# Down projection in four groups of output tiles, one visit behind each pair of up tiles

## The chip, the cores and the metric

The kernel runs on one core of one Trainium2 chip. The metric is the device time of one execution in microseconds (us). TensorE multiplies matrices, VectorE and ScalarE do elementwise work, GpSimd and SyncE mostly issue transfers, and sixteen DMA engines move the data. In the profile these are PE (PEld is its weight load), DVE, ACT, POOL and SP.

## The reference

One layer of a decoder on 512 prompt tokens and 8 x 4 sample tokens, all in float32. The part that matters here is the second half of the layer.

```python
x = x + g1 * (jnp.concatenate([a_out, o], axis=-1) @ p['w_out'])
h2 = rms_norm(x, p['norm_ffn_g']) * (1 + sc2) + sh2
u, f_tail = causal_dwconv(f_prev, h2 @ p['w_up'], p['ffn_conv_w'], p['ffn_conv_b'])
gate, val = jnp.split(u, 2, axis=-1)
x = x + g2 * ((jax.nn.silu(gate) * val) @ p['w_down'])
```

D_MODEL is 2048 and D_FF is 5632. The six modulation vectors (`sh1` ... `g2`) are `silu(c) @ w_ada + b_ada`. The convolution has three taps along the tokens.

## The kernel before

Channels lie on the 128 partitions, tokens on the free axis: 544 columns as two halves of 272 (256 prompt tokens and 16 sample tokens each). Every float32 product is made of three float32r matmuls: weights and operands are split into a rounded part and a rest, `hi` by a ScalarE cast (L353) and `lo` by a VectorE subtraction (L354), and `hi*hi`, `hi*lo` and `lo*hi` are summed in PSUM. A weight unit of 512 KB (128 x 1024) is loaded by SyncE into a ring of five buffers (`raw_w` three, `raw_x` two), and `split_w` (L199) splits half of it at a time into a ring of three `whi` and three `wlo`.

Entry. While the output projection (`rest`, L832) runs, SyncE loads the weights of the last modulation stage, which holds the gate `g2`, into `raw_g`; the sixteen steps of the stage (`ada_stage`, L268) come after it, six ahead of the sum of squares and ten behind. `normalized` (L879) scales two channel tiles of x at a time, `blocks` (L894) splits them into the operands B1 and B2. The first two pairs of up tiles (a gate tile f and its value tile 44+f) are made by plain products (`direct`, L936), with 192 matmuls a pair. `combine` (L899) makes the operands T1, T2, T3 and T4.

Up. The other 42 pairs use seven products (`product`, L1025) in place of eight, 24 matmuls of 272 columns each. `up_mm` (L1035) loads four units, forms four weight combinations on VectorE (L1045 to L1047, L1055) and adds the products up from five PSUM banks (pool `psf`, four buffers, `bank`) into `usg` and `usv`. `gated_act` (L1083) then makes the convolution, silu, the product and the split of the result; five results are kept.

Down. `down(c)` (L1105) takes four K tiles (a chunk) and all sixteen output tiles m: 24 matmuls per m into one of two PSUM pairs (`main_ps`), an eviction that multiplies by the gate (ScalarE L1118, VectorE L1119) into a ring `ym` of three, and a GpSimd transfer that adds `ym` to `o_y[m]` in memory (L1120). The order of work is four pairs, with `down(c-1)` behind the first of them, eleven times:

```python
for j in range(2 if c == 0 else 0, CHUNK):
    up_pair(CHUNK * c + j, st_in, tails, j)
    ...
    if c and j == 0:
        down(c - 1)
```

Copies of the two window caches (128 of 1 MB, memory to memory, L924) are issued behind some of the weight loads (`shift_cache`). The program is written in this order, and a scheduler that estimates when each instruction becomes ready sets the final order on every engine's queue; engines take their queues strictly in that order. `tc.issue_after(ins)` fixes that an instruction comes behind `ins` on the engine of `ins`.

Of the kernel before, what the change touches and what calls it, by code (L numbers as in the profile page):

```python
# [60 lines left out]
YM = 3  # L61
# [3 lines left out]
              [(48 + k, 64 + k, 4) for k in (0, 4, 8, 12)] + [(80, 84, 4), (88, 92, 4)])  # L65
D2D = (PAST - DT) * DC // 8
# [53 lines left out]
def build(ctx, tc, A):  # L120
# [147 lines left out]
    def ada_stage(psp, tmp, s, loaded=None, banks=None):  # L268
# [3 lines left out]
        ps = banks[:, 0] if banks is not None else psp.tile([P, 512], F32, name="x", bufs=XB)  # L272
# [15 lines left out]
        pt = banks[:, 1] if banks is not None else psp.tile([P, 512], F32, name="m")  # L288
# [543 lines left out]
    def rest():  # L832
# [4 lines left out]
        for m in range(2, KT):  # L837
            ps = main_ps()
            for h in range(1 if m < 8 else 0, 2):
                mm_unit(ps, A["w_out"][m, h], mhi, mlo, 8 * h, h == 0 or m < 8, h == 1)  # L840
                yield
# [52 lines left out]
    def blocks(h, j, n):  # L894
        src = x2[h][:, j:j + n].rearrange("p k c n -> p c k n")
        hi, lo = (b[:, :, j:j + n] for b in (B1, B2)[h])
        split(hi, lo, src)
# [52 lines left out]
    for j in range(0, 4, 2):  # L950
        normalized(0, j, 2)
# [25 lines left out]
    def us_tile(st_in, slot):  # L977
        us = fe.tile([P, UW], F32, name="us", bufs=2)
        seg = us[:, USEG:].rearrange("p (b w) -> p b w", w=2 + DT)
        nc.gpsimd.memset(us[:, 0:2], 0.0)  # L980
        nc.gpsimd.tensor_copy(seg[:, :, 0:2], st_in[:, slot])
        return us
# [19 lines left out]
    def placed(outs, st_in, j):  # L1002
        uss = [us_tile(st_in, 2 * j + i) for i in range(2)]
        for us, out in zip(uss, outs):
            for c in range(2):
                place(us, c, copied, out[c])
        return uss

    st_in = state_tile(0)
    us0 = placed(first, st_in, 0)  # L1010
    second = [main_ps(), main_ps()]
# [6 lines left out]
    direct(1, [[t[:, c] for c in range(2)] for t in second], while_sums)  # L1018
# [16 lines left out]
    def up_mm(f, usg, usv):  # L1035
        a11, _ = load_u(A["w_up"][f, 0])
# [85 lines left out]
    for c in range(NCHUNK):  # L1122
        if c:
            st_in = state_tile(c)
# [134 lines left out]
```

## Time and profile before

| | us |
|---|---|
| Three runs: median (lowest to highest) | 2735.04 (2724.3 to 2739.17) |
| Profiled execution, own time | 2729.78 |
| Its span | 2728.0 |
| TensorE busy in the span | 2583.4 |
| VectorE busy | 1677.4 |
| ScalarE busy | 1258.3 |
| Mean granted TensorE clock, share of full | 0.982 |

The span runs from the first to the last instruction of the profiled execution. Busy time of TensorE has modelled ends, so it says how long matmuls were in flight and not how fast they went. "A <- B" in a row means that A stood idle until B was done.

### The profile page before, as it was taken

Reading aid. Unit: us, or ns where it says so; the run is one execution under the profiler, and the core shown is the slowest. Engines: PE = TensorE matmul, PEld = TensorE weight load, DVE = VectorE, ACT = ScalarE, POOL = GpSimd, SP = SyncE. Lnnn points to the kernel's source line nnn. Section 1 sums busy time; section 2 is a strip of 40 time slices with the busy share of each in tenths; the row PEclk is TensorE's granted clock in tenths of the full one; section 3 lists DMA queues with packets and bytes.
Section 4 is the critical chain, followed back from the end, with each engine's and each line's share of the span. In section 5 each row is a group of like instructions: output and inputs, shape, how many; then the busy total and the mean of one; then the engine's idle time right before and its main releaser. Section 6 shows DMA issues by size and latency. Waiting matters only on the chain.

```text
span 2728.0 us, 51730 instructions
## 1 busy us (share of the span) xinstructions
PE 2583.4 (95%) x20597; PEld 2342.4 (86%) x20597; DVE 1677.4 (61%) x3029; ACT 1258.3 (46%) x2371; POOL 332.4 (12%) x624
## 2 busy tenths in 40 slices
PE   6999999999999999799999999999999999999998
PEld 5878677768777789699999999999999999999998
DVE  4678654644665333785767667585748484848573
ACT  4355455444455322554444445454435454544443
POOL 0000000000000000012121211112121212121212
PEclk8999999999999999899999999999999999999999
DMA  9884557676756453448576776767585849585856
GB/s 347 273 274 156 194 196 259 221 258 230 245 190 216 150 203 131 156 163 224 184 225 183 228 202 212 202 205 205 211 202 199 215 180 246 188 238 176 244 169 107
DMA packets 144482, 566.53 MB, mean 208 GB/s; under 512 B 18544, under 2 KB 28400, under 8 KB 141424
## 3 DMA queue, kind: packets, MB, share of 16 engines
q1 hardware_dynamic: 103744, 494.98, 52.4%
q0 software_dynamic: 25344, 49.03, 11.8%
q10 hardware_dynamic: 15152, 19.22, 2.0%
q8 instruction: 161, 2.64, 0.4%
q14 instruction: 81, 0.66, 0.1%
HBM read 503.18 MB, written 193.94 MB: 256 GB/s over the span
## 4 chain that ended last, share of the span: by engine, by line
PE 67%; DVE 12%; DMA 10%; issue 6%; ACT 3%; POOL 1%; SPq 0%; DVEq 0%; ACTq 0%; POOLq 0%
PE acc L209 38%; PE b L933 18%; DVE wlo L354 4%; DMA raw_w<-w_up 4%; PE x L280 3%; DMA o_y<-ym 3%; DMA raw_x<-w_up 2%; ACT whi L353 2%; DVE ca L1078 2%; PE x L714 2%; PE x L665 2%; PE m L523 1%; DVE us L992 1%; ACT ca L1076 1%; DMA raw_g<-w_ada 1%
## 5 line engine op out<-in xcount | busy, mean ns | idle before, releaser
L353 ACT CAST whi<-raw_w 128x512 fp32r<-128x512 f32 x650 | 399.2, 619 | 694.4 <-PE acc L209 468.3
L354 DVE TENSOR_TENSOR wlo<-raw_w,whi 128x512 fp32r<-128x512 f32 x650 | 443.0, 689 | 414.4 <-ACT whi L353 404.3
L209 PE MATMUL acc<-hhi,whi 128*128 128x272 f32 x1792 | 394.9, 299 | 10.8 <-ACT whi L353 6.7
L209 PE MATMUL acc<-hhi,wlo 128*128 128x272 f32 x1792 | 383.3, 293 | 0.1
L209 PE MATMUL acc<-hlo,whi 128*128 128x272 f32 x1792 | 381.8, 293 | 0.0
L209 PEld LDWEIGHTS acc<-hhi,whi 128*128 128x128 f32 x1792 | 284.0, 190 | 61.2 <-issue 40.2
L209 PE MATMUL acc<-ahi,whi 128*128 128x272 f32 x1408 | 297.9, 294 | 29.0 <-DVE ym L1119 27.9
L209 PEld LDWEIGHTS acc<-hhi,wlo 128*128 128x128 f32 x1792 | 285.0, 190 | 22.7 <-issue 20.9
L209 PEld LDWEIGHTS acc<-hlo,whi 128*128 128x128 f32 x1792 | 284.4, 190 | 21.0 <-issue 18.5
L209 PE MATMUL acc<-alo,whi 128*128 128x272 f32 x1408 | 295.1, 291 | 0.0
L209 PE MATMUL acc<-ahi,wlo 128*128 128x272 f32 x1408 | 294.3, 291 | 0.0
L353 ACT CAST whi<-raw_x 128x512 fp32r<-128x512 f32 x270 | 165.7, 620 | 235.8 <-PE b L933 115.1
L354 DVE TENSOR_TENSOR wlo<-raw_x,whi 128x512 fp32r<-128x512 f32 x270 | 183.2, 687 | 121.9 <-ACT whi L353 119.6
L209 PEld LDWEIGHTS acc<-ahi,whi 128*128 128x128 f32 x1408 | 224.4, 192 | 33.7 <-DVE ym L1119 32.5
L209 PEld LDWEIGHTS acc<-alo,whi 128*128 128x128 f32 x1408 | 225.3, 192 | 0.2 <-DVE alo L354 0.2
L209 PEld LDWEIGHTS acc<-ahi,wlo 128*128 128x128 f32 x1408 | 224.8, 191 | 0.0
L933 PE MATMUL b<-b2hi,whi 128*128 128x272 f32 x704 | 205.8, 292 | 9.9 <-ACT whi L353 9.9
L933 PE MATMUL b<-b2hi,wlo 128*128 128x272 f32 x704 | 205.8, 293 | 8.7 <-DVE wlo L354 8.6
L933 PE MATMUL b<-b1hi,wlo 128*128 128x272 f32 x704 | 205.5, 295 | 2.2 <-DVE wlo L354 2.2
L933 PE MATMUL b<-b1hi,whi 128*128 128x272 f32 x704 | 204.0, 292 | 1.3 <-ACT whi L353 1.0
L933 PE MATMUL b<-b1lo,whi 128*128 128x272 f32 x704 | 204.6, 292 | 0.1
L933 PE MATMUL b<-b2lo,whi 128*128 128x272 f32 x704 | 203.3, 289 | 0.0
(253 smaller groups left out, 5175.1 us busy)
## 6 DMA issues: line engine op xcount, KB each, us to landing
raw_s<-w_ada SPq DMA_DIRECT2D x176, 512.0 KB, 4.8
o_k_s<-cache_k SPq DMA_DIRECT2D x64, 1022.0 KB, 7.1
o_v_s<-cache_v SPq DMA_DIRECT2D x64, 1022.0 KB, 6.9
raw_w<-w_up SPq DMA_DIRECT2D x109, 512.0 KB, 4.3
o_y<-ym POOLq DMA_DIRECT2D x176, 272.0 KB, 5.2
raw_w<-w_in SPq DMA_DIRECT2D x80, 512.0 KB, 4.5
raw_x<-w_up SPq DMA_DIRECT2D x67, 512.0 KB, 4.3
raw_s<-kT_c SPq DMA_DIRECT2D x64, 448.0 KB, 4.4
```

What stands on the lines that cost most here:

```text
L209: nc.tensor.matmul(out[:, c, 0:HALF], lhsT=w, rhs=x[:, c, :], start=start and i == 0, stop=stop and i == 2)
L280: nc.tensor.matmul(ps[32 * j:32 * j + 9, 0:w], lhsT=silc[:, kt, :], rhs=t[:, c:c + w], start=kt == 0, stop=kt == KT - 1)
L353: nc.scalar.copy(hi, src)
L354: return nc.vector.tensor_tensor(lo, src, hi.bitcast(F32), op=ALU.subtract).ins
L523: nc.tensor.matmul(o_ps[rows[par], 0:P], lhsT=vt[:, kj, rows[par]], rhs=pts[par][:, P * kj:P * kj + P], start=kj == 0, stop=kj == qi, skip ...
L665: nc.tensor.matmul(s_ps[32 * g:32 * g + 32, 0:hk], lhsT=qb[:, 2 * g + o, n, :], rhs=ks[g], start=o == 0 and n == 0, stop=o == 1 and n == 1 ...
L714: nc.tensor.matmul(o_ps[32 * g:32 * g + 32, :], lhsT=pT[0:w, c0:c0 + 32], rhs=rhs[g], start=kt == 0, stop=kt == 7)
L933: nc.tensor.matmul(out[:, 0:HALF], lhsT=w, rhs=x, start=start and i == 0, stop=stop and i == 2, skip_group_check=True)
L992: nc.vector.tensor_tensor(out, ps, t, op=ALU.add)
L1076: nc.scalar.activation(acc, us[:, 0:UN], AF.Identity, bias=fw[:, m, 3:4], scale=fw[:, m, 0:1])
L1078: nc.vector.scalar_tensor_tensor(acc, us[:, j:j + UN], fw[:, m, j:j + 1], acc, op0=ALU.mult, op1=ALU.add)
```

## The change

The down projection is cut into 47 visits of four output tiles. Visit v takes group v mod 4 (tiles 4g to 4g+3) and K tiles up to v, at most four; the first three and the last three visits have fewer. After pair f the program makes visit f-1, and between its two weight units it loads three units of pair f+1 and forms two of its weight combinations. After the last pair four visits are left. The units are padded with zeros to full size.

In `up_mm` the products run in another order (B11, B21, T2, T1, T3, B22, T4), three banks take all seven (b1 four times, b3 twice), and partial results go from PSUM to SBUF by ScalarE copies. `usg` and `usv` are two fixed tiles, their sample heads written by ScalarE. The ring `ym` shrinks from three to two.

At the entry, one load of the last modulation stage is issued behind each weight load of the output projection from the seventh on, six steps of the stage run inside the projection, and five ahead of the sum. Normalisations other than the first two are issued behind splits on VectorE. The first direct pair uses the PSUM pairs of `main_ps`, the second the banks, and pair 2 borrows the former.

```diff
-YM = 3
+YM = 2
...
+VISITS = ([(f % CHUNK, max(0, f + 1 - CHUNK), min(f + 1, CHUNK)) for f in range(FT)] +
+          [(g, FT - CHUNK + g + 1, CHUNK - 1 - g) for g in range(CHUNK - 1)])
...
-    raw_g = []
+    raw_g = deque()
     loads = ada_loads(last_ada, lambda: og.tile([P, 1024], F32, name="raw_g"))
-    for i, _ in enumerate(rest()):
-        if i >= 10 and len(raw_g) < RAW_G:
-            raw_g.append(next(loads))
-
-    ada = ada_stage(psf, op, last_ada, chain(raw_g, loads), main_ps())
-    for _ in range(6):
+
+    def loaded():
+        while True:
+            yield raw_g.popleft()
+
+    ada = ada_stage(psf, op, last_ada, loaded(), [psf.tile([P, 512], F32, name="b") for _ in range(2)])
+    for i, ins in enumerate(rest()):
+        if ins is not None and i >= 6:
+            if i >= 18:
+                next(ada)
+            with tc.issue_after(ins):
+                t = next(loads, None)
+            if t is not None:
+                raw_g.append(t)
+
+    for _ in range(5):
...
+    todo = deque((h, j) for h in range(2) for j in range(0, 8, 2))
+    for _ in range(2):
+        normalized(*todo.popleft(), 2)
 
     def plain(h, u):
-        for j in (0, 2):
-            blocks(h, 4 * u + j, 2)
-            if (h, u) != (1, 1):
-                normalized(h + u, 4 * (1 - u) + j, 2)
-
-    first = [[bank(), bank()] for _ in range(2)]
-    direct(0, first, plain)
+        for j in (4 * u, 4 * u + 2):
+            ins = blocks(h, j, 2)
+            if todo:
+                with tc.issue_after(ins):
+                    normalized(*todo.popleft(), 2)
+
+    first = [main_ps(), main_ps()]
+    direct(0, [[t[:, c] for c in range(2)] for t in first], plain)
...
+    us = [f32(fe, [P, UW], n, bufs=1) for n in ("usg", "usv")]
+    for t in us:
+        nc.gpsimd.memset(t[:, 0:2], 0.0)
+
+    def segments(t):
+        return t[:, USEG:].rearrange("p (b w) -> p b w", w=2 + DT)
+
+    def open_us(st_in, j):
+        for i, t in enumerate(us):
+            nc.scalar.copy(segments(t)[:, :, 0:2], st_in[:, 2 * j + i])
...
-    def up_mm(f, usg, usv):
-        a11, _ = load_u(A["w_up"][f, 0])
-        a21, _ = load_u(A["w_up"][FT + f, 0])
-        a22, ins = load_u(A["w_up"][FT + f, 1])
+    def up_weights(f):
+        g0, _ = load_u(A["w_up"][f, 0])
+        v0, _ = load_u(A["w_up"][FT + f, 0])
+        v1, ins = load_u(A["w_up"][FT + f, 1])
         shift_cache(ins)
+        s1 = fe.tile([P, 2, 4, P], F32, name="sum", bufs=1)
+        nc.vector.tensor_tensor(s1, v0, v1, op=ALU.add)
+        nc.vector.tensor_tensor(v0, g0, v0, op=ALU.subtract)
+        return g0, v0, v1, s1
+
+    def up_mm(f, b1, b2, b3):
+        a11, s3, a22, s1 = weights.pop(f)
+        usg, usv = us
         a12, ins = load_u(A["w_up"][f, 1])
         shift_cache(ins)
-        s1 = fe.tile([P, 2, 4, P], F32, name="sum", bufs=1)
-        b1 = bank()
         product(b1, a11, B11, True, True)
-        nc.vector.tensor_tensor(s1, a21, a22, op=ALU.add)
-        nc.vector.tensor_tensor(a21, a11, a21, op=ALU.subtract)
-        nc.vector.tensor_tensor(a11, s1, a11, op=ALU.subtract)
-        b2 = bank()
-        product(b2, a11, T2, True, True)
         p1 = part_tile("p1", 2)
         nc.scalar.copy(p1, b1[:, 0:HALF])
+        nc.vector.tensor_tensor(a11, s1, a11, op=ALU.subtract)
+        product(b2, a12, B21, True, True)
+        nc.vector.tensor_tensor(a12, a12, a11, op=ALU.subtract)
+        place(usg, 0, plus, b2, p1)
+        product(b1, a11, T2, False, True)
         u2 = part_tile("u2")
-        plus(u2, b2[:, 0:HALF], p1)
-        product(b1, a12, B21, False, True)
-        nc.vector.tensor_tensor(a12, a12, a11, op=ALU.subtract)
-        place(usg, 0, copied, b1)
-        product(b2, a21, T3, False, True)
+        nc.scalar.copy(u2, b1[:, 0:HALF])
+        product(b3, s1, T1, True, True)
+        p5 = fp.tile([P, HALF], F32, name="p5", bufs=1)
+        nc.scalar.copy(p5, b3[:, 0:HALF])
+        product(b1, s3, T3, False, True)
         u3 = part_tile("u3")
-        plus(u3, b2[:, 0:HALF], p1)
-        b3 = bank()
-        product(b3, s1, T1, True, True)
-        plus(u2, b3[:, 0:HALF], u2)
-        place(usv, 1, plus, b3, u3)
-        b4 = bank()
-        product(b4, a12, B22, True, True)
-        place(usg, 1, plus, b4, u2)
-        b5 = bank()
-        product(b5, a22, T4, True, True)
-        place(usv, 0, plus, b5, u3)
+        nc.scalar.copy(u3, b1[:, 0:HALF])
+        place(usv, 1, plus, p5, u3)
+        product(b3, a12, B22, False, True)
+        place(usg, 1, plus, b3, u2)
+        product(b1, a22, T4, False, True)
+        place(usv, 0, copied, b1)
...
-    def down(c):
-        for mp in range(8):
-            raw, ins = load_u(A["w_down"][c, mp])
-            if mp % 2:
+    def down(v, between=lambda: None):
+        g, k0, n = VISITS[v]
+        for q in range(2):
+            raw, ins = load_u(A["w_down"][v, q])
+            if q:
                 shift_cache(ins)
             for j in range(2):
-                m = 2 * mp + j
+                m = 4 * g + 2 * q + j
                 hi, lo = split_w(raw[:, j])
                 ps = main_ps()
-                for k in range(CHUNK):
-                    ahi, alo = acts[CHUNK * c + k]
-                    mm3(ps, hi[:, k, :], lo[:, k, :], ahi, alo, k == 0, k == CHUNK - 1)
+                for k in range(n):
+                    ahi, alo = acts[k0 + k]
+                    mm3(ps, hi[:, k, :], lo[:, k, :], ahi, alo, k == 0, k == n - 1)
                 ym = fp.tile([P, 2, HALF], F32, name="ym", bufs=YM)
                 nc.scalar.activation(pv(ym), pv(ps), AF.Copy, scale=modT[:, G2 + m, 0:1])
                 nc.vector.tensor_tensor(sv4(ym), sv4(ps), per_batch(modT[:, G2 + m, 1:9]), op=ALU.mult)
                 nc.gpsimd.dma_start(A["o_y"][m], ym, accum_op=ALU.add)
-
-    for c in range(NCHUNK):
-        if c:
-            st_in = state_tile(c)
-        tails = fe.tile([P, 2 * CHUNK, 9, 2], F32, name="tails", bufs=2)
-        if c == 0:
-            gated_act(0, *us0, tails, 0)
-        for j in range(2 if c == 0 else 0, CHUNK):
-            up_pair(CHUNK * c + j, st_in, tails, j)
-            if c == 0 and j == 2:
-                gated_act(1, *placed([[t[:, i] for i in range(2)] for t in second], st_in, 1), tails, 1)
-            if c and j == 0:
-                down(c - 1)
-        nc.scalar.dma_start(A["o_fc"][c], tails)
-    down(NCHUNK - 1)
+            if not q:
+                between()
+
+    weights = {2: up_weights(2)}
+    tails = [None]
+
+    def tails_tile():
+        tails[0] = fe.tile([P, 2 * CHUNK, 9, 2], F32, name="tails", bufs=2)
+
+    tails_tile()
+    gated_act(0)
+    placed(second, st_in, 1)
+    gated_act(1)
+    for f in range(2, FT):
+        if f % CHUNK == 0:
+            st_in = state_tile(f // CHUNK)
+            tails_tile()
+        open_us(st_in, f % CHUNK)
+        if f == 2:
+            t, t3 = main_ps(), main_ps()
+            up_mm(f, t[:, 0], t[:, 1], t3[:, 0])
+        else:
+            up_mm(f, bank(), bank(), bank())
+        gated_act(f)
+        if f % CHUNK == CHUNK - 1:
+            nc.scalar.dma_start(A["o_fc"][f // CHUNK], tails[0])
+        if f == 2:
+            down(0)
+
+        def ahead():
+            if f + 1 < FT:
+                weights[f + 1] = up_weights(f + 1)
+
+        down(f - 1, ahead)
+    for v in range(FT - 1, len(VISITS)):
+        down(v)
```

## Rows read from the trace of the kernel before

**Rows 1.** Page, part 1: busy time, share, instructions of each engine.

```profile
PE 2583.4 (95%) x20597; PEld 2342.4 (86%) x20597; DVE 1677.4 (61%) x3029; ACT 1258.3 (46%) x2371; POOL 332.4 (12%) x624
```

**Rows 2.** Timelines of ScalarE and GpSimd, the last output tiles.

```profile
2716.13 0.69 ACT L1118 ACTIVATE ym<-acc,modT 128x512 f32<-128x512 f32 x1 [2.32 <-PE acc L209]
2719.13 0.69 ACT L1118 ACTIVATE ym<-acc,modT 128x512 f32<-128x512 f32 x1 [2.32 <-PE acc L209]
...
2720.34 0.86 POOL L1120 DMA_DIRECT2D o_y<-ym  x1 [2.14 <-DVE ym L1119]
```

**Rows 3.** Table by stage: length; busy PE, PEld, DVE, ACT, POOL; clock, DMA share, GB/s.

```profile
1280.00:1300.00 20.00, 17.70 (x129) 17.49 (x128) 6.35 (x12) 6.75 (x12) 4.31 (x5) 0.91 0.95 251
1303.48:1394.14 90.66, 86.23 (x668) 84.39 (x667) 74.46 (x127) 46.34 (x83) 12.31 (x28) 1.00 0.55 192
1394.14:1447.37 53.23, 51.23 (x393) 50.57 (x393) 20.15 (x42) 21.11 (x35) 14.34 (x20) 0.97 0.98 236
```

**Rows 4.** Waits of TensorE, 1165 to 2728 us: total, times, longest.

```profile
PE b L933 <- ACT whi L353: 35.1, 53, 1.0
PE acc L209 <- DVE ym L1119: 27.9, 17, 4.5
```

**Rows 5.** Groups by line and shape, 1250 to 2728 us.

```profile
L354 DVE TENSOR_TENSOR wlo<-raw_w,whi 128x512 fp32r<-128x512 f32 x388 | 263.2, 687 | 197.1 <-ACT whi L353 194.0
L353 ACT CAST whi<-raw_w 128x512 fp32r<-128x512 f32 x388 | 237.9, 620 | 354.0 <-PE acc L209 164.7 <-PE b L933 160.3 <-issue 21.4
...
L933 PE MATMUL b<-t2hi,whi 128*128 128x272 f32 x312 | 94.5, 303 | 22.2 <-ACT whi L353 22.2
...
L1119 DVE TENSOR_TENSOR ym<-acc,modT 128x32 f32<-128x32 f32 x176 | 32.6, 185 | 52.9 <-ACT ym L1118 52.9
...
L1045 DVE TENSOR_TENSOR sum<-raw_w,raw_x 128x1024 f32<-128x1024 f32 x16 | 19.6, 1226 | 21.8 <-DMA raw_x<-w_up 21.6
```

**Rows 6.** Timeline of all engines at one T2 product.

```profile
1638.85 1.21 DVE L1047 TENSOR_TENSOR raw_x<-sum,raw_x 128x1024 f32<-128x1024 f32 x1
...
1640.55 0.39 ACT L1051 COPY p<-b 128x272 f32<-128x272 f32 x1 [0.58 <-PE b L933]
1640.83 1.14 ACT L353 CAST whi<-raw_x 128x512 fp32r<-128x512 f32 x2
...
1641.51 0.39 PE L933 MATMUL b<-t2hi,whi 128*128 128x272 f32 x1 [0.99 <-ACT whi L353]
```

**Rows 7.** Timelines of VectorE and TensorE at one late eviction.

```profile
1428.31 1.23 DVE L1045 TENSOR_TENSOR sum<-raw_w,raw_x 128x1024 f32<-128x1024 f32 x1 [2.33 <-DMA raw_x<-w_up]
...
1429.69 0.58 PE L209 MATMUL acc<-ahi,whi 128*128 128x272 f32 x2 [1.84 <-DVE ym L1119]
```

**Rows 8.** DMA issues, 2695 to 2715 and 1394 to 1447; then all landings.

```profile
o_y<-ym POOLq DMA_DIRECT2D x8, 272.0 KB, 4.0
...
o_y<-ym POOLq DMA_DIRECT2D x15, 272.0 KB, 6.0
...
DMA to landing us min/median/max: 3.9/5.2/10.3
```

**Rows 9.** The entry: modulation matmuls (first and last start), then timelines of three engines.

```profile
L280 PE MATMUL acc<-raw_g,cin x128: 378/379/386, 1096.2 to 1108.1; 128*9 128x256 f32 x128
...
1105.99 0.73 DVE L314 SCALAR_TENSOR_TENSOR ssum<-w 128x544 f32<-128x544 f32 x1
...
1108.97 9.68 DVE L883 TENSOR_TENSOR half<-half,ssum 128x1088 f32<-128x1088 f32 x8
...
1119.14 3.37 DVE L889 TENSOR_TENSOR half<-half,modT 128x32 f32<-128x32 f32 x32
...
1110.27 11.39 ACT L891 ACTIVATE half<-half,modT 128x512 f32<-128x512 f32 x16 [0.84 <-DVE half L883]
...
1122.08 1.10 ACT L353 CAST b1hi<-half 128x1088 fp32r<-128x1088 f32 x1
...
1123.23 1.28 PE L933 MATMUL b<-b1hi,whi 128*128 128x272 f32 x4 [0.38 <-ACT b1hi L353]
```

More of the change, by code (lines that the diff above doesn't have):

```diff
@@ L271, in ada_stage @@
         per = 1024 // (groups * w)
-        ps = banks[:, 0] if banks is not None else psp.tile([P, 512], F32, name="x", bufs=XB)
+        ps = banks[0] if banks is not None else psp.tile([P, 512], F32, name="x", bufs=XB)
         loaded = loaded or ada_loads(s, raw_tile)
@@ L287, in ada_stage @@
             copy(st[32 * j:32 * j + 9, 0:w], ps[32 * j:32 * j + 9, 0:w])
-        pt = banks[:, 1] if banks is not None else psp.tile([P, 512], F32, name="m")
+        pt = banks[1] if banks is not None else psp.tile([P, 512], F32, name="m")
         ns, nj = w // P, groups // 2
@@ L839, in rest @@
             for h in range(1 if m < 8 else 0, 2):
-                mm_unit(ps, A["w_out"][m, h], mhi, mlo, 8 * h, h == 0 or m < 8, h == 1)
-                yield
+                yield mm_unit(ps, A["w_out"][m, h], mhi, mlo, 8 * h, h == 0 or m < 8, h == 1)
             gated(m, ps, op)
@@ L896, in blocks @@
         hi, lo = (b[:, :, j:j + n] for b in (B1, B2)[h])
-        split(hi, lo, src)
+        return split(hi, lo, src)
     def combine(j, n):
@@ L975, in load_u @@
         return load_w(src)
[L977 to L982, printed above, removed]
+    us = [f32(fe, [P, UW], n, bufs=1) for n in ("usg", "usv")]
[6 more added lines that the diff above has]
+            nc.scalar.copy(segments(t)[:, :, 0:2], st_in[:, 2 * j + i])
     def place(us, c, op, ps, t=None):
@@ L1002, in placed @@
     def placed(outs, st_in, j):
-        uss = [us_tile(st_in, 2 * j + i) for i in range(2)]
-        for us, out in zip(uss, outs):
+        open_us(st_in, j)
+        for t, out in zip(us, outs):
             for c in range(2):
-                place(us, c, copied, out[c])
-        return uss
+                place(t, c, copied, out[c])
     st_in = state_tile(0)
-    us0 = placed(first, st_in, 0)
-    second = [main_ps(), main_ps()]
+    placed([[t[:, c] for c in range(2)] for t in first], st_in, 0)
+    second = [[bank(), bank()] for _ in range(2)]
     sums = chain(combine(0, 4), combine(4, 4))
@@ L1016, in while_sums @@
             next(sums, None)
-    direct(1, [[t[:, c] for c in range(2)] for t in second], while_sums)
+    direct(1, second, while_sums)
     run(sums)
@@ L1071, in up_conv @@
     def up_conv(m, us, tails, slot):
-        seg = us[:, USEG:].rearrange("p (b w) -> p b w", w=2 + DT)
         nc.gpsimd.tensor_copy(tails[:, slot, 0, :], us[:, SEQ:SEQ + 2])
-        nc.gpsimd.tensor_copy(tails[:, slot, 1:9, :], seg[:, :, DT:DT + 2])
+        nc.gpsimd.tensor_copy(tails[:, slot, 1:9, :], segments(us)[:, :, DT:DT + 2])
         acc = fp.tile([P, UN], F32, name="ca", bufs=2)
@@ L1081, in build, with gated_act @@
     acts = {}
-    def gated_act(f, usg, usv, tails, j):
-        gt = up_conv(f, usg, tails, 2 * j)
-        vl = up_conv(FT + f, usv, tails, 2 * j + 1)
+    def gated_act(f):
+        j = f % CHUNK
+        gt = up_conv(f, us[0], tails[0], 2 * j)
+        vl = up_conv(FT + f, us[1], tails[0], 2 * j + 1)
         nc.scalar.activation(gt, gt, AF.Silu)
@@ L1195 @@
     w_up = units(I["w_up"][0], np.arange(UT))
-    w_down = I["w_down"][0].reshape(NCHUNK, CHUNK, P, 8, 2, P).transpose(0, 3, 2, 4, 1, 5)
-    w_down = np.ascontiguousarray(w_down.reshape(NCHUNK, 8, P, 8 * P))
+    wd = I["w_down"][0].reshape(FT, P, 4, 2, 2, P)
+    w_down = np.zeros((len(VISITS), 2, P, 2, CHUNK, P), np.float32)
+    for v, (g, k0, n) in enumerate(VISITS):
+        w_down[v, :, :, :, 0:n] = wd[k0:k0 + n, :, g].transpose(2, 1, 3, 0, 4)
+    w_down = w_down.reshape(len(VISITS), 2, P, 8 * P)
     sa = I["state_conv_a"][0].transpose(2, 0, 1).reshape(CT, P, DB, 30)
```

6 lines of the change are left out of this document (removed).

## The prediction

> **What bounds the kernel now.** I read the page first, then tables by stage, waits, groups by shape, timelines and transfers. TensorE is busy 95% of the span, VectorE 61%, ScalarE 46% [rows 1]. So the span is the matmul stream plus its holes, and the reader should look for the holes. The change leaves the number of matmuls alone: 168 per pair of up tiles (seven products of 24), 24 per output tile and four K tiles, 4224 in the whole down projection before and after.
>
> The pace of an undisturbed stream stands at the very end, where evictions of 24 matmuls each start at 2716.13 and 2719.13 us: 3.00 us a tile, 125 ns a matmul [rows 2]. Against it stands one chunk in the steady part. Four up pairs take 90.66 us for 668 recorded matmuls, which at 125 ns are 83.5; the down chunk takes 53.23 us for 393, which are 49.1 [rows 3]. So a pair loses 1.8 us and sixteen output tiles 4.1. What the waits name fits: in the feed-forward part TensorE stands 35.1 us in 53 waits for ScalarE's casts in the up products, and 27.9 us in 17 waits for VectorE to evict an output tile [rows 4]. (The waits come out smaller than the losses because the modelled end of a matmul overlaps the hole.)
>
> The groups by shape place the first kind: 22.2 us of it stands before the T2 product [rows 5]. A timeline shows one. VectorE makes the T2 operand until 1640.06 (L1047); ScalarE, which could cast it then, has the copy of p1 in front (L1051), which first waits for a product to end; the casts start at 1640.83 and T2 at 1641.51, after 0.99 us of idleness [rows 6]. T2 is the second product, so its operand, two dependent VectorE operations away from the loads, is needed 3 us after the pair begins.
>
> The second kind: at 1428.31 VectorE starts `sum` of the next pair after standing 2.33 us for its weights. The small part of an eviction (L1119) comes behind it on VectorE, and TensorE waits 1.84 us for it [rows 7].
>
> **The change, part by part.** The sum is made against the profiled execution's own 2729.78 us, 5 us under the median.
>
> *Up order.* Sums for pair f+1 (two of the four 1.22 us VectorE operations, [rows 5]) move into the down visit before it, T2 becomes the third product, and its last subtraction needs only `s1` and the casts of product one. A12's product, whose weights need no arithmetic, stands second. From the start of the pair to T2 there are then 6 us in place of 3; the work between (1.22 us, a cast of 0.62, a subtraction of 0.69 [rows 5]) fits. Three result banks replace five: b1 takes products one, three, five and seven, b3 four and six. Every reuse has one product of 24 matmuls, 3.0 us, between, in which ScalarE must make one copy; such a copy is 0.39 us [rows 6]. ScalarE gains three copies a pair and VectorE loses three additions. Neither is near full: four pairs and sixteen tiles hold 74.5+20.2 = 94.6 us of VectorE in 143.9, ScalarE 67.5 [rows 3]. I expect most of the 1.8 us to go and keep 0.4 for what I can't see: 1.4 x 42 pairs = **-59 us**. Bounds: all of it, -76; half of it, -38.
>
> *Down in visits.* Evictions grow from 176 to 188, splits from 176 to 188, weight units from 88 to 94 (padded with zeros). That is 12 more of 0.69+0.62 us on ScalarE and of 0.69+0.19 on VectorE [rows 2, 5], hidden under matmuls in the steady part. Four tiles now follow each pair, so VectorE's surplus of the up stretch (74.5 us of 90.7) is spread over the slack of the down stretch (20.2 of 53.2), and o_y accumulations come 4 in 33 us, no longer 16 in 53, where the DMA share was 0.98 [rows 3]. Against that, the sums of every pair now fall into a visit, where before only one pair in four had them there; and the ring `ym` shrinks from three to two. A slot comes back after 1.21 us to the DMA's issue (2719.13 to 2720.34, [rows 2]) plus the landing: 4.0 us alone, 6.0 in a down stretch, 3.9 to 10.3 overall, median 5.2 [rows 8]. So the cycle is 5.2 to 11.5 us, typically 6.5. The third eviction of a visit comes 6 us after the first, so it waits 0.5 us. No later tile needs the accumulator before the next pair is through; the wait reaches TensorE only through ScalarE, where the next pair's casts queue behind. The fourth eviction starts cycle - 6 us after its tile's end, takes 0.69, and a cast of 0.62 stands behind it; `whi` has three buffers, two of them filled by then, which is 3 us of matmuls. So the cover ends at a cycle of about 7.5 us. For the longer cycles and the sums' waits I take 1.0 us a visit, what four tiles lose now (4.1/4): **0 us**; bounds 0.3 us (-29) and 2.0 us (+41).
>
> *The first short visits.* At f = 2 visits 0 and 1 come together: four tiles of 6 matmuls, four of 12, 9 us of matmuls. Two ym buffers at a cycle of 6.5 us pass a tile each 3.25 us, and two accumulators let TensorE run two tiles ahead: the sixth eviction starts some 15 us in, so TensorE leaves after about 18. **+9 us**, 4 to 14 by cycles of 5.2 and 8.
>
> *The last short visits.* Visits 44 to 46 have K lengths 3, 2 and 1: 2.25, 1.5 and 0.75 us a tile, with no pair behind them to fill the wait. By the undisturbed cycle (1.21+4.0 us for two tiles, 2.6 a tile) the excess is 4 x (0.35+1.1+1.85) = **+13 us**; at 6.0 us landing, 3.6 a tile, it would be 25.
>
> *The entry.* Now RMSNorm's factor is ready at 1106.72; then all eight multiplications (9.68 us) and sixteen activations (11.39 us) run before the first cast of B1 at 1122.08, and the first up matmul comes at 1123.23 [rows 9]. After, only two calls go before: 1.21 us, four activations of 0.71 and a cast of 1.10, 5.2 us. Six of sixteen steps of the last modulation stage (128 matmuls in 11.9 us, [rows 9]) move into the output projection; that is 4.4 us earlier and no saving by itself. The last output matmul now ends near 1096.3, 10.4 us before the factor: 1096.3+4.4+10.4+5.2 = 1116.3, 7 us earlier. Some returns: a normalisation is 1.6 us (1.21 and four small operations, 3.37/8), two blocks' subtraction 1.2, and so VectorE needs 7 us with the weight splits for the 6 us of matmuls of four k, +4 over 16 k; the T sums then press on the second direct pair. **-3 us**, -9 to +3.
>
> Sum: -59+0+9+13-3 = -40: 2690 us beside 2729.78, **2695 us** beside the median of 2735. Half a per cent, 14 us, is about what a measurement here can tell from no change.
>
> **The rivals.**
> 1. *The ring of two decides* (slower). Each visit stops TensorE for the cycle minus 7.5 us; at the busy stretch's landing of 6.0 the cycle is 7.2, and nothing is lost. It takes the gain back when a visit loses 2.0 us, at a cycle of 9.5. At a landing of 9 us (cycle 10.3) a visit loses 2.8, and the sum is -40+1.8 x 41 = +34: 2769 us. For it: three copies of 1 MB per pair still run, near the visits. Against: landings are mostly 5.2, and the queue is less crowded. Chance 0.09.
> 2. *The clock.* In 1280 to 1300 us, where evictions stopped TensorE, the granted clock is 0.91; in the up stretch, whose holes are at most 1 us, 1.00 [rows 3]. If each visit brings such a dip, 9% of 20 us, 1.8 us x 41 = 74: 2769 us. The stretches named show no such dip behind short holes, so I give it 0.03. The Trainium skill, "TensorE: Matmul & The Clock Gate", under "A second HAM failure mode: psum-queue depth-cycling", tells of a kernel that paused briefly between groups of matmuls in PSUM and kept falling back to the lower of the two levels, 1.2 GHz. By that rule the visits would pay it; by the up stretch's 1.00 they would not.
> 3. *The up holes stay*: the four copies wait on ScalarE for products' ends as p1 does now, casts behind them. Then the -59 goes: 2754 us. For it: [rows 6] shows just that order. Against: the cast behind is needed a product later. Chance 0.07.
> 4. *All holes go*, 0.1 us a pair and 0.3 a visit: another -13 and -29: 2653 us. Chance 0.19.
>
> **The numbers.** Forecast 0.62, of it 0.54 beyond half a per cent and 0.08 within; rival 4 wholly faster; 1 to 3 slower by 0.06, 0.02 and 0.05, the rest within. Faster 0.73, same 0.14, slower 0.13. The range takes in rival 4 and, above, the forecast's dear ends, and leaves most of 1 and 2 out: 2648 to 2748.
>
> **What would show it.** Right: no wait before T2 in the groups by shape; a pair with its visit in 33 to 34.5 us (264 x 125 ns is 33.0; now 36.0); b1's reuse without waits; ym waits on o_y in most visits, but with little TensorE idle behind; some 30 us or more for the last twelve tiles; the first up matmul near 1116. Wrong: TensorE waiting for casts at the start of each pair behind a ym wait (rival 1), a granted clock below 0.97 in the steady part (2), holes of 0.5 to 1 us at product ends (3). Landing times of o_y in visits are what I know least.

## The result, and the profile after

The changed kernel takes 2649.08 us (median of 4 runs, 2645.43 to 2652.55); the kernel before, run beside it, 2735.82. The ratio is 0.969, 95% interval 0.967 to 0.972: 3.1% faster, where 1.5% was forecast. The direction was right and the time lies at the lower edge of the range; the gain was twice the forecast's. The profiled execution took 2652.55 us, its span 2650.8: 77.2 us less than before.

Part 1 of the page after, against [rows 1]: TensorE is 32 us less in flight, VectorE 15 us less busy, ScalarE 68 us busier.

```profile
PE 2551.4 (96%) x20597; PEld 2322.5 (88%) x20597; DVE 1662.5 (63%) x2927; ACT 1326.0 (50%) x2609; POOL 275.0 (10%) x462
```

The table by stage after, columns as in [rows 3]: the first short visits, two pairs with their visits, the whole steady part, the tail.

```profile
1190.00:1225.00 35.00, 21.52 (x144) 19.43 (x142) 18.62 (x34) 16.57 (x32) 8.24 (x11) 0.85 0.83 223
1251.75:1285.43 33.68, 33.46 (x266) 33.15 (x265) 22.91 (x40) 18.75 (x36) 5.66 (x8) 1.00 0.79 227
1285.43:1319.11 33.68, 33.68 (x271) 33.68 (x270) 23.16 (x39) 18.58 (x36) 5.30 (x9) 1.00 0.74 221
1251.75:2560.00 1308.25, 1297.62 (x10279) 1292.68 (x10278) 897.18 (x1520) 704.39 (x1327) 199.44 (x312) 1.00 0.77 221
2579.00:2643.00 64.00, 49.72 (x365) 47.12 (x363) 22.67 (x50) 28.46 (x46) 18.24 (x23) 0.92 0.82 134
```

A pair with its visit is 264 matmuls and takes 33.7 us; in [rows 3] four pairs and sixteen tiles took 143.9 us, 36.0 each. The granted clock is 1.00 over the steady part. In these rows it is low where TensorE stands long: 0.85 in the short visits, 0.92 in the tail.

Waits of TensorE, 1165 to 2651 us, against [rows 4]: the 35.1 us on `whi` are 4.1, while the waits on `ym` kept their sum.

```profile
PE acc L211 <- DVE ym L1132: 29.5, 25, 6.8
PE b L944 <- ACT whi L355: 4.1, 9, 0.5
...
PE b L944 <- DVE wlo L356: 1.1, 3, 0.7
```

The group of the T2 product, which had 22.2 us of idleness before it in [rows 5], has none:

```profile
L944 PE MATMUL b<-t2hi,whi 128*128 128x272 f32 x320 | 92.7, 290 | 0.0
```

And ScalarE's waits, 1100 to 2651 us and so with both ends in them, show the ring of two at work:

```profile
ACT ym L1131 <- DMA o_y<-ym: 117.8, 65, 4.4
```

**A ledger by equal work.** Stages are compared by what they lose: length less number of matmuls times 0.1253 us, the pace of undisturbed stretches (3.01 us for 24; [rows 2] give 3.00). The first part runs from the first up matmul to where every pair has a full tile count behind it (before: to the first chunk, 888 matmuls; after: to pair 4, 864). The steady part then goes to the last up matmul (10392 and 10464), the tail to the end (384 and 336). In the kernels with visits 8 to 12 matmuls of pair 4 run ahead of this border, so 1.0 to 1.5 us of the first part's loss there belong to the steady part.

| | before | after | difference | forecast |
|---|---|---|---|---|
| output projection ends at | 1096.2 | 1090.3 | -5.9 | +4.4 |
| from there to the first up matmul | 27.0 | 16.5 | -10.5 | -11.4 |
| first part (from 1123.23; 1106.76), loss | 14.6 | 36.7 | +22.1 | +13 |
| steady part (from 1249.07; 1251.75), loss | 116.9 | 19.6 | -97.3 | -59 |
| tail (from 2668.1; 2582.45), loss | 11.8 | 26.2 | +14.4 | +13 |
| sum | | | -77.2 | -40 |

So two lines were missed by much: the steady part by 38 us, the projection's end by 10. The first part cost 9 us more than forecast.

The clock has a share in the steady part's line. Before, that part ran at 0.99 of the full clock:

```profile
1249.07:2668.10 1419.03, 1348.97 (x10395) 1326.12 (x10393) 926.33 (x1648) 661.77 (x1139) 263.10 (x472) 0.99 0.70 207
```

The trace shows the lower of the two levels (1.2 GHz) in eight places of it, 34 us together: six came behind output tiles whose first matmul was 2.0 to 4.7 us late, two behind an up pair with matmuls 1.2 and 0.7 us late. At half the clock that is at most 17 of the 116.9 us (an estimate). After the change there is no such place.

### The profile page after: what moved, and what is told of

It is laid out like the page before. It is cut to its first block, busy times and chain, and to the rows that moved or that the text cites. A ratio compares the mean times of both kernels' runs of the same rounds, so it can differ in the third digit from the quotient of the medians.

```text
span 2650.8 us, 51546 instructions
## 1 busy us (share of the span) xinstructions
PE 2551.4 (96%) x20597; PEld 2322.5 (88%) x20597; DVE 1662.5 (63%) x2927; ACT 1326.0 (50%) x2609; POOL 275.0 (10%) x462
## 3 DMA queue, kind: packets, MB, share of 16 engines
q0 software_dynamic: 27072, 52.38, 14.4%
## 4 chain that ended last, share of the span: by engine, by line
PE 86%; DMA 5%; issue 4%; DVE 3%; ACT 1%; POOL 1%; POOLq 0%; ACTq 0%; DVEq 0%; SPq 0%
PE acc L211 43%; PE b L944 31%; PE x L282 4%; PE x L716 2%; PE x L667 2%; DMA raw_s<-w_ada 1%; DMA raw_w<-w_up 1%; PE m L525 1%; DMA o_y<-ym 1%; DVE wlo L356 1%; PE acc L944 1%; PE m L455 1%; POOL o_y L1133 1%; PE m L490 1%; PE m L487 1%
## 5 line engine op out<-in xcount | busy, mean ns | idle before, releaser
L355 ACT CAST whi<-raw_w 128x512 fp32r<-128x512 f32 x654 | 404.9, 620 | 606.8 <-PE acc L211 395.7
L356 DVE TENSOR_TENSOR wlo<-raw_w,whi 128x512 fp32r<-128x512 f32 x654 | 449.4, 691 | 392.3 <-ACT whi L355 372.9
L355 ACT CAST whi<-raw_x 128x512 fp32r<-128x512 f32 x278 | 172.3, 620 | 201.1 <-PE b L944 111.6
L356 DVE TENSOR_TENSOR wlo<-raw_x,whi 128x512 fp32r<-128x512 f32 x278 | 191.6, 690 | 126.0 <-ACT whi L355 125.2
L1133 POOL DMA_DIRECT2D o_y<-ym x188 | 162.9, 867 | 499.2 <-DVE ym L1132 491.8
L944 PE MATMUL b<-b2hi,wlo 128*128 128x272 f32 x688 | 198.9, 290 | 0.2 <-DVE wlo L356 0.2
L944 PE MATMUL b<-b2hi,whi 128*128 128x272 f32 x688 | 199.1, 290 | 0.0
L944 PE MATMUL b<-b1hi,wlo 128*128 128x272 f32 x688 | 198.5, 289 | 0.3 <-DVE wlo L356 0.2
L944 PE MATMUL b<-b2lo,whi 128*128 128x272 f32 x688 | 197.9, 288 | 0.0
```

What stands on the lines that cost most here:

```text
L355: nc.scalar.copy(hi, src)
L356: return nc.vector.tensor_tensor(lo, src, hi.bitcast(F32), op=ALU.subtract).ins
L944: nc.tensor.matmul(out[:, 0:HALF], lhsT=w, rhs=x, start=start and i == 0, stop=stop and i == 2, skip_group_check=True)
L1133: nc.gpsimd.dma_start(A["o_y"][m], ym, accum_op=ALU.add)
```

## The experiments

Two theories for the steady part. A: the order of the up products, with the sums made ahead, closes the holes of the pairs, as forecast. B: the visits close them, because VectorE's surplus of one pair falls under the visit's matmuls. A third question is what the ring of two costs, a fourth what moved the projection's end. Effects of 5 to 15 us are near what the times resolve, so the trace's stages are read beside them. The kernel before had a median of 2741.14 us beside e1 to e4, of 2735.45 beside c1 and e5 to e7, and of 2737.25 beside e8 to e11; kernels that ran beside different medians are compared by their ratios to it. A stage's loss is read from one profiled execution; c1 and e7 below repeat two of them, and differ from the first by 2 and 7 us.

**c1**, the changed kernel again, as a control.

> The changed kernel itself, for a comparison on one chip with the other three. Both theories expect the ratio found before, 0.969 (0.966 to 0.972).

2648.59 us, ratio 0.9685 (0.9652 to 0.9718). Its losses are 34.5, 17.9 and 26.5 us in the three parts. Its steady part by stage and by TensorE's waits:

```profile
1249.24:2578.31 1329.07, 1320.79 (x10459) 1315.41 (x10457) 910.46 (x1546) 715.31 (x1347) 201.15 (x317) 1.00 0.77 220
```

```profile
PE acc L211 <- DVE ym L1132: 3.9, 5, 0.9
PE b L944 <- ACT whi L355: 3.6, 9, 0.5
PE b L944 <- DVE wlo L356: 0.4, 2, 0.2
```

### Order, sums ahead and visits

**e3**: the old order of products, sums still ahead.

```diff
...
         product(b1, a11, B11, True, True)
+        nc.vector.tensor_tensor(a11, s1, a11, op=ALU.subtract)
+        product(b2, a11, T2, True, True)
         p1 = part_tile("p1", 2)
...
-        product(b2, a12, B21, True, True)
...
+        product(b1, a12, B21, False, True)
...
```

> The changed kernel with the products of up_mm in the order of before (T2 second), five accumulations in four banks and VectorE additions, but with the two sums still formed ahead. Theory that the order removes the hole before T2: about 1 us a pair comes back, 2680 to 2695 us. Rival, that the sums formed ahead removed it: at most 10 us, 2649 to 2660.

2662.53 us, 0.9718 (0.9686 to 0.9751); the steady part loses 23.2 us, 5 more than c1. By the ratio that is 9 us slower than c1, near the rival's forecast.

**e4**: the new order, but loads and sums at the start of the pair.

```diff
...
         open_us(st_in, f % CHUNK)
+        if f > 2:
+            weights[f] = up_weights(f)
...
         def ahead():
-            if f + 1 < FT:
-                weights[f + 1] = up_weights(f + 1)
+            return
...
```

> The changed kernel with the three loads and two sums of a pair at that pair's start, not in the visit before it; the new order of products stays. Theory that loads and sums ahead are what the pairs needed: 1 us or more a pair, 2685 to 2700 us. Rival, that the order alone does it (the first product needs no sum, the second no arithmetic): within 10 us of 2649.

2660.06 us, 0.9711 (0.9681 to 0.9741); the steady part loses 31.0 us, 13 more than c1; by the ratio it is 7 us slower, again as the rival had it. In both the edit that was undone cost far less than the -59 us laid on the pair of them. Either each suffices alone, or neither is what matters. The next two runs part these.

**e5**: order and sums both undone (`up_mm` as before, but with T4 in bank b1 and the two fixed tiles `usg` and `usv`), visits kept.

```diff
...
-        a11, s3, a22, s1 = weights.pop(f)
+        a11, _ = load_u(A["w_up"][f, 0])
+        s3, _ = load_u(A["w_up"][FT + f, 0])
+        a22, ins = load_u(A["w_up"][FT + f, 1])
+        shift_cache(ins)
...
+        nc.vector.tensor_tensor(s1, s3, a22, op=ALU.add)
+        nc.vector.tensor_tensor(s3, a11, s3, op=ALU.subtract)
+        nc.vector.tensor_tensor(a11, s1, a11, op=ALU.subtract)
+        product(b2, a11, T2, True, True)
...
```

> The changed kernel with the whole old form of an up pair: old product order, weight loads and sums at the pair's start, five results; the down projection stays in visits. Theory A (order and sums ahead each close the holes of a pair, so that undoing one alone costs only 11 to 13 us, and undoing both opens them again): 2690 to 2710 us, with waits of the cast of a weight on DVE in front of TensorE of 25 to 45 us over 42 pairs. Theory B (the visits close the holes, because VectorE no longer has four tiles' worth of eviction and casts in a row behind it when the pair begins): 2660 to 2672 us, the sum of what the two edits cost alone, and waits on VectorE's casts and sums under 15 us.

2676.41 us, 0.9786 (0.9751 to 0.9821): between the two forecasts, 4 us above B's and 14 below A's, and without waits on VectorE's `wlo`. The steady part, by stage and by TensorE's waits:

```profile
1254.24:2602.01 1347.77, 1327.31 (x10454) 1318.17 (x10453) 952.06 (x1664) 684.08 (x1229) 229.61 (x317) 1.00 0.76 217
```

```profile
PE b L944 <- ACT whi L355: 15.6, 31, 0.5
PE acc L211 <- DVE ym L1137: 4.7, 7, 1.3
```

It loses 36.6 us, 0.9 for a pair and its visit, where the kernel before lost 116.9 with the same order.

**e6**: order and sums as changed, the down projection in chunks as before, with `ym` of three and `p1` of one. Where no chunk follows a pair, the next pair's loads and sums come straight behind it.

```diff
...
-    def down(v, between=lambda: None):
-        g, k0, n = VISITS[v]
-        for q in range(2):
...
+    def down(c, between):
+        for mp in range(8):
...
-        down(f - 1, ahead)
...
+        if f >= CHUNK and f % CHUNK == 0:
+            down(f // CHUNK - 1, ahead)
+        else:
+            ahead()
...
```

> The changed kernel with its new order of products and its sums ahead, but with the down projection as before: all 16 output tiles behind every fourth pair, three buffers of ym (p1 has one buffer to make room). Theory A (order and sums ahead close the holes of the up pairs): the up pairs lose 0.4 us each, the visits' short tiles and the longer tail fall away, and only the 16 tiles in a row wait on the ring (2660 to 2675 us; the waits on ym at TensorE 28 us as before). Theory B (the visits do it): three pairs in four run without a visit in front of them and still show holes; 2690 to 2715 us.

2676.23 us, 0.9789 (0.9748 to 0.983): between the two forecasts, 1 us above A's and 14 below B's. The steady part loses 78.2 us. By stage: the whole, four pairs, and sixteen tiles; then TensorE's waits in the whole:

```profile
1233.90:2614.18 1380.28, 1332.66 (x10395) 1316.06 (x10393) 881.22 (x1531) 708.90 (x1334) 237.15 (x316) 1.00 0.73 212
...
1427.20:1513.99 86.79, 84.96 (x667) 84.06 (x666) 69.64 (x117) 50.60 (x98) 11.21 (x16) 1.00 0.59 200
1513.99:1566.03 52.04, 49.67 (x394) 49.12 (x392) 20.06 (x41) 21.63 (x39) 13.27 (x16) 1.00 0.96 238
```

```profile
PE acc L211 <- DVE ym L1131: 23.3, 20, 3.2
PE b L944 <- DVE wlo L356: 18.4, 30, 0.9
PE b L944 <- ACT whi L355: 5.3, 9, 1.0
```

The same part before had these:

```profile
PE b L933 <- ACT whi L353: 32.1, 48, 1.0
PE acc L209 <- DVE ym L1119: 26.8, 16, 4.5
PE b L933 <- DVE wlo L354: 10.8, 26, 1.4
```

The new order did take away most of the waits on `whi`, but the pairs now wait more on `wlo`, VectorE's subtraction (18.4 us for 10.8), and the chunks still wait on `ym`. VectorE's row shows why the pairs do: 69.6 us busy in 86.8 of pairs (80%), 20.1 in 52.0 of tiles (39%). The timeline of VectorE at the start of one pair (from its 2425.30 on VectorE does not stop for eleven us) has the convolution of the last pair (L1094), sums (L1057, L1058), combinations (L1069, L1071) and the subtractions that TensorE waits for, all in one queue:

```profile
2425.30 1.22 DVE L1057 TENSOR_TENSOR sum<-raw_w,raw_x 128x1024 f32<-128x1024 f32 x1
2426.43 0.69 DVE L356 TENSOR_TENSOR wlo<-raw_w,whi 128x512 fp32r<-128x512 f32 x1
2427.04 0.80 DVE L1094 SCALAR_TENSOR_TENSOR ca<-usv,fw,ca 128x560 f32<-128x560 f32 x1
...
2430.20 1.22 DVE L1069 TENSOR_TENSOR raw_x<-sum,raw_x 128x1024 f32<-128x1024 f32 x1
2431.33 0.68 DVE L1105 TENSOR_TENSOR a<-ca 128x512 f32<-128x512 f32 x1
...
2432.45 1.22 DVE L1071 TENSOR_TENSOR raw_w<-raw_w,raw_x 128x1024 f32<-128x1024 f32 x1
```

In the visits kernel the same work is spread: 22.9 and 23.2 us in 33.7 for every pair (68 and 69%, table above). The losses of the steady part as a square:

| steady loss, us | chunks | visits |
|---|---|---|
| old order, sums in the pair | 116.9 (before) | 36.6 (e5) |
| new order, sums ahead | 78.2 (e6) | 17.9 (c1) |

Order and sums take 39 us in chunks and 19 in visits; the visits take 80 or 60. (The kernel before also lacks the fixed `usg` and `usv`, so 60 and 19 are the cleaner differences. e6 has three buffers of `ym` and one of `p1`; the same buffers in visits, e8 below, lose 15.9, so they are not what holds e6 back. e7, whose steady part is that of the kernel before, loses 109.5 there: the first cell is known to some 7 us.)

So both theories hold a part, and the visits do more, but not only by what B names. From e6 to c1 the waits on `wlo` in the pairs fall by 18 us, which is B's; the waits on `ym` in the output tiles fall by 19, which is another matter. The starts of the matmuls say the same. If each step from one start to the next, less 0.1253 us, is put to the matmul that ends it, the steady part's loss parts so:

| | before | e6 | e5 | c1 |
|---|---|---|---|---|
| ahead of up matmuls | 74.6 | 47.7 | 28.8 | 12.8 |
| ahead of matmuls of output tiles | 42.3 | 30.5 | 9.4 | 6.2 |

Some of this is the clock: the lower level stands for 34 us in the kernel before, 14 in e6, 3 in e5 and not at all in c1, at most half of that in loss. It can be up to 7 of the 60 us and up to 15 of the 80. Why evictions in chunks come late is seen in places ([rows 7]: VectorE stood for a weight load with the eviction behind it), but no run parts the causes.

### The ring

**e8**: three buffers of `ym`.

```diff
...
-YM = 2
+YM = 3
...
-        p1 = part_tile("p1", 2)
+        p1 = part_tile("p1")
...
```

> The changed kernel with three buffers of ym instead of two (p1 has one buffer to make room). Theory A (the ring of two holds up the short visits at both ends and nothing between, since its 65 waits on ScalarE in the steady part lie under TensorE's work): the waits of acc on ym at TensorE fall from 24 us in 18 to about 10 us, the time by 8 to 15 us to 2634 to 2641 us, steady pair and visit still lose 0.45 us. Theory B (at the ends it is the transfers themselves, not the buffers: a third one only lengthens the queue): within 4 us of 2649 us, with o_y landing later than the median of 4.9 us. Rival of the prediction (the ring prices each steady visit at 1.0 us): 30 us or more off.

2636.48 us, 0.9641 (0.9614 to 0.9667). In the steady part ScalarE's waits for `o_y` go altogether (c1: 84.2 us in 43), and the loss goes from 17.9 to 15.9: the ring of two cost 2 us there, not 1.0 us a visit. The tail goes from 68.6 to 60.1 us. The time is theory A's, but the first part stays (34.7, c1 34.5), against it.

**e9**: from the visit behind the last pair on, every second result through the two free buffers of `ca`.

```diff
...
-                ym = fp.tile([P, 2, HALF], F32, name="ym", bufs=YM)
+                if v >= FT - 1 and (2 * q + j) % 2:
+                    ym = fp.tile([P, UN], F32, name="ca", bufs=2)[:, 0:2 * HALF].rearrange("p (c n) -> p c n", c=2)
+                else:
+                    ym = fp.tile([P, 2, HALF], F32, name="ym", bufs=YM)
...
```

> The changed kernel in which, from the visit behind the last pair on, every second tile's result goes through the two free buffers of ca, so that four results can be under way there. Theory A (the ring is what stretches the tail): the tail behind the last matmul of the up projection falls from 68.5 us to 55 to 60 us and the time to 2637 to 2642 us. Theory B (the engines' evictions and the transfers set the pace): tail 64 us or more, time within 5 us of 2649 us.

2638.14 us, 0.9648 (0.9625 to 0.9672); the tail is 57.8 us, as theory A had it. Its stretch of matmuls in c1 (56 us) and in e9 (47 us):

```profile
2578.00:2634.00 56.00, 46.03 (x339) 43.70 (x338) 19.64 (x43) 24.97 (x41) 15.93 (x19) 0.96 0.83 133
```

```profile
2581.00:2628.00 47.00, 44.27 (x340) 43.15 (x339) 19.02 (x44) 25.21 (x42) 15.93 (x19) 0.97 0.92 155
```

The same work moves at 155 GB/s in place of 133; a transfer of `o_y` lands after 5.3 us in the median (c1: 4.3), but four may be under way.

**e10**: e8 and e9 together.

> Both edits together: three buffers of ym throughout and the two of ca in the tail. If the ring is what costs at both ends, the gains add up where they are in different places: first short visits 8 us shorter, tail 10 us shorter, 2628 to 2637 us. If the transfers set the pace: 2644 to 2652 us.

2632.42 us, 0.9632 (0.9607 to 0.9656), the fastest version here: by the ratios 14 to 16 us under the changed kernel (the two intervals just touch; the runs themselves, 2629.57 to 2638.4, lie apart from c1's 2647.76 to 2650.29). The tail is 56.8 us, the first part unmoved (33.8).

**e11**: without the cache copies, so that two outputs stay unwritten where they are copied.

```diff
...
-    copies = [(n, b, i) for n in "kv" for b in range(DB) for i in range(8)]
+    copies = []
...
```

> The changed kernel without the copies of the old cache rows to its outputs (o_k_s and o_v_s stay unwritten where they are copied). Theory A (the result transfers of the first short visits land late because of the other traffic, 0.83 of the DMA engines busy there): o_y lands in under 4 us in the median instead of 4.9, the waits of acc on ym between 1190 and 1225 us fall from 12 us to under 5, and the time by 8 us or more. Theory B (the pace of the ring is the transfer's own length and ScalarE's part of the eviction): within 4 us of 2649 us, and the waits stay.

2638.31 us, 0.9646 (0.9622 to 0.9669). The steady part loses 6.8 us in place of 17.9, which is where the time comes from; the tail stays (68.8). The 24 us from the first matmul of the first short visits, in c1, e8 and e11 in turn, each with the landing of the `o_y` issued around there:

```profile
1192.27:1216.27 24.00, 14.31 (x88) 12.92 (x87) 13.25 (x24) 11.66 (x22) 5.70 (x7) 0.79 0.95 280
...
DMA to landing us min/median/max: 4.1/4.9/9.5
```

```profile
1190.27:1214.27 24.00, 14.47 (x84) 12.95 (x83) 13.36 (x24) 11.19 (x22) 4.84 (x6) 0.79 0.93 280
...
DMA to landing us min/median/max: 4.0/7.2/11.9
```

```profile
1197.39:1221.39 24.00, 18.15 (x116) 16.78 (x115) 15.55 (x29) 13.83 (x28) 6.75 (x9) 0.86 0.87 168
...
DMA to landing us min/median/max: 4.1/4.2/5.6
```

With a third buffer alone the transfers only land later (7.2 for 4.9 us), and no more matmuls get through; without the copies they land in 4.2 us, and 28 more do. So here the busy DMA engines (0.95) stretch the ring's cycle, and theory A holds in kind: from this first matmul to pair 4 it takes 57.0 us in c1 and 51.5 in e11. The clock is in it too: at 0.79 over 24 us it takes up to 5 us of the visits in c1 (an estimate, 0.21 x 24). But the first part as a whole loses 32.7 us (c1 34.5), since the pairs ahead of these visits took 3.8 us longer in e11. Their rows, c1 and e11, differ in the clock:

```profile
1106.52:1192.27 85.75, 76.83 (x552) 74.25 (x553) 72.71 (x109) 54.04 (x92) 7.42 (x13) 0.94 0.41 145
```

```profile
1107.87:1197.39 89.52, 78.90 (x553) 76.08 (x554) 72.95 (x109) 54.09 (x92) 6.82 (x13) 0.90 0.25 80
```

0.06 of 85.75 us and 0.10 of 89.52 are 5.1 and 9.0 us, so the clock accounts for most or all of the 3.8 (an estimate). What three buffers and no copies would do together is open.

### The entry

**e1**: the twelve loads of the last modulation stage in one burst again, and its steps in the program behind the output projection.

```diff
...
+    for i, _ in enumerate(rest()):
+        if i >= 10 and len(raw_g) < RAW_G:
+            raw_g.append(next(loads))
...
-        if ins is not None and i >= 6:
-            if i >= 18:
-                next(ada)
-            with tc.issue_after(ins):
-                t = next(loads, None)
...
```

> The changed kernel with the weight loads of the last modulation stage issued as before the change (twelve from the eleventh unit on, without an order behind the unit loads) and its steps behind the output projection. Theory: the entry gained about 10 us because a burst of twelve 512 KB loads no longer holds up the output projection's own weights, so this gives 8 to 11 us back: 2657 to 2661 us, with TensorE waits for casts near 950 to 985 us. Rival: the entry gained only by the order of the normalisations; then the time stays within 3 us of 2649.

2661.88 us, 0.9713 (0.9676 to 0.9749). Its last matmul of the projection starts at 1097.99 us, 8.1 later than after (1089.89), and the steady part 9.2 later. But e1 does not test the burst alone. The scheduler set 104 of the stage's 128 matmuls into the projection, from 954 to 991 us, where after has 40 (1056 to 1084), so more work stands in front of that end, and the first up matmul comes only 4.8 us later. The time is the theory's; the cause is left to e7.

**e7**: the kernel before, with these loads alone spread.

```diff
...
-        if i >= 10 and len(raw_g) < RAW_G:
-            raw_g.append(next(loads))
+        if ins is not None and i >= 12:
+            with tc.issue_after(ins):
+                t = next(loads, None)
...
```

> The kernel before with one edit alone: the twelve early loads of modulation weights are issued one behind each unit load of the output projection, not all at once. Theory A (the burst held up the output projection's own weights): 8 to 10 us faster than the kernel before (ratio 0.9965), the projection ends 8 to 10 us earlier, and the waits of acc on the cast of whi between 880 and 1100 us (6.7 us) go. Theory B (the earlier end in the changed kernel came with the modulation steps inside the projection, not with the loads): within 3 us of the kernel before.

2721.78 us, 0.9949 (0.9928 to 0.997). The modulation stage, which follows the projection, starts at 1088.5, 7.7 us earlier than in [rows 9], and TensorE's 6.7 us of waits for the cast of `whi` are gone, both as theory A had it. The 20 us of the burst and the 30 behind them, in the kernel before and in e7:

```profile
950.00:970.00 20.00, 15.47 (x109) 15.04 (x109) 6.22 (x15) 4.12 (x7) 0.00 (x0) 0.91 1.02 416
970.00:1000.00 30.00, 27.18 (x203) 26.73 (x202) 12.84 (x26) 7.91 (x13) 0.00 (x0) 0.94 0.49 170
```

```profile
950.00:970.00 20.00, 19.30 (x137) 18.91 (x138) 9.70 (x21) 5.93 (x10) 0.00 (x0) 0.91 0.63 230
970.00:1000.00 30.00, 30.00 (x241) 30.00 (x240) 13.98 (x27) 9.54 (x15) 0.00 (x0) 1.00 0.44 145
```

Twelve loads at once filled the DMA engines (1.02, 416 GB/s) and landed late (12.3 us in the median), the projection's own weights among the traffic: 28 matmuls fewer in the same 20 us, and 38 fewer in the next 30. Together that is 8.3 us at 0.1253 us each. Theory A holds. How far one trace tells the projection's end is seen in the runs whose entry is that of the changed kernel: it lies between 1085.3 us (e10) and 1095.1 (e9).

**e2**: `normalized` put in the program ahead of the blocks, without its place behind them.

```diff
...
-                with tc.issue_after(ins):
-                    normalized(*todo.popleft(), 2)
+                normalized(*todo.popleft(), 2)
...
```

> The changed kernel with the normalisations not fixed behind the splits. Theory: all eight run before the first cast of B1 again, the first up matmul comes some 8 us later, and most of it stays lost: 2654 to 2658 us. Rival: VectorE has the same work to do before the first two pairs are through, so what starts later catches up; within 3 us of 2649.

2653.39 us, 0.9687 (0.9654 to 0.972): no difference that the times resolve. In the trace the first up matmul comes 25.3 us after the projection's last one starts (after: 16.9), with 14.6 us of waiting for `b1hi` (6.1); the first part is then 142.6 us (after 144.8, c1 142.7). The span is 3.3 us longer than after. In e2 the projection happened to end 3.4 us earlier than after, which hides part of the delay: from its last matmul to the end of the first part it takes 167.9 us (after 161.9, c1 159.6). So the trace keeps 6 to 8 us of the delay, as the theory had it, and the times do not resolve it.

## Why the prediction was wrong in its size

- **Down in visits, "0 us"**: this is the step that failed, outside its own bounds (-29 to +41). Measured, the visits take 60 us from the steady part beside the new order, 80 beside the old. The prediction priced only new costs, the ring and the sums, and kept for them the 1.0 us a visit that four tiles lost before. In c1 output tiles lose 6.2 us ahead of their matmuls, 0.16 a visit. The old loss was one of sixteen tiles in a row: in chunks, e6's tiles still lose 30.5 us (before: 42.3). Part of it was the clock: 0.97 over 53.23 us in [rows 3] is up to 1.6 of the 4.1 us. The queue of transfers (0.98 of the DMA engines there, 0.77 after) is likely another part, which no run shows by itself. The visits also take some 35 us from the up pairs (47.7 to 12.8); the prediction named what does it (VectorE's surplus of the up stretch falls into the slack of the down stretch) and gave it no price.
- **The ring of two**: right in its mechanism, wrong in its size. In c1's steady part ScalarE waits 84 us for a buffer, and TensorE 3.9 us for an eviction, as the argument of the cover said; a third buffer gives back 2 us there. Rival 1 is out.
- **Up order, -59 us**: near in its sum, by luck in part. Up pairs lose 62 us less in c1 than before. But order and sums alone take 27 of it from them (74.6 to 47.7), 39 from the steady part, at the bound of -38, because VectorE's subtractions (`wlo`) become the next limit in pairs without a visit. The order does remove the wait before T2, as forecast. That part of rival 3 was near: holes stayed, though on VectorE and not on ScalarE's copies.
- Together: -59 and 0 were forecast, -97 measured. A pair and its visit lose 0.45 to 0.49 us, where the forecast kept 1.4 and rival 4 0.4. Rival 4's steady part is what happened, and it had 0.19.
- **Rival 2, the clock**: out as a loss. The granted clock is 1.00 over 1308 us of visits. It belongs in the sum with the other sign: the kernel before had 34 us at the lower level in its steady part, up to 17 us of loss, which the forecast took for part of the chunks' holes. The Trainium skill ("TensorE: Matmul & The Clock Gate", "A second HAM failure mode: psum-queue depth-cycling") tells of a kernel whose frequent short pauses between groups of matmuls brought the lower level again and again. The waits left here, at most 0.9 us long in c1's steady part, brought none.
- **The entry, -3 us**: -12.4 measured, -5.9 and -10.5 with 4.0 given back. From the projection's end to the first up matmul 15.6 us were forecast and 16.5 came. The 4 us given back fit too: e6, whose entry is that of the changed kernel, loses 18.6 us in its first part, before 14.6. Missed was the end of the projection, 10 us: the loads that the diff spreads were costed at nothing, although they were issued in a burst beside the projection's own. e7 (-7.7) measures the term.
- **The first short visits, +9 us**: 15.9 in c1 (34.5 less e6's 18.6; 14.9 without the border's 1.0), beyond the bound of 14. The cycle of 6.5 us was taken from a landing of 5.2; the landings there reach 9.5, with the DMA engines at 0.95. The clock, 0.79 over the first 24 us of them, had no term; it takes up to 5 us.
- **The last short visits, +13 us**: 14.4 measured. Right, and e9 shows its cause: with four buffers 10.8 us of it go.

## What to carry to other kernels

Where two stages alternate, one with a full side engine and one with a slack one, look at the side engine's share in each stage and not over the span: cutting both into short turns gave here more than the better order inside the full stage, and a stage's old loss is no estimate for the new arrangement. A load that is issued early is not free: ask what else is loading in those microseconds, and issue one behind each load that it would delay. Count result buffers where tiles are short, not where they are long: the ring of two cost 2 us in 1329 us of full visits and 8 to 11 in the last 69. In the first short visits, beside full DMA engines, a third buffer gave nothing.

## What the hardware showed that was not expected

A burst of twelve loads of half a megabyte held the DMA engines at 1.02 of their time and 416 GB/s and set the matmuls beside it and behind it back by some 8 us (e7). And more result transfers under way gave no more rate in the first short visits, where loads and copies share the engines (280 GB/s with two buffers and with three; landings of 4.9 and 7.2 us), while in the tail they did (133 to 155 GB/s).
